# Three slots for the modulation weights of the mixing stages, one of them taken from the LRU gates' ring

## The chip, the cores and the metric

One core of a Trainium2 chip runs the program. The metric is the device time of one execution in microseconds (us); a lower time is better. The engines are TensorE (PE in the profile, its weight loads PEld), VectorE (DVE), ScalarE (ACT), GpSimd (POOL) and SyncE (SP), whose queue issues most of the transfers. Profile and runs are those of the kernel before the change.

## What is computed

A diffusion backbone of two layers over 512 latent tokens and 256 context tokens of 1024 features, all in float32. Every layer mixes tokens in two parallel groups (an S5 state-space group and a gated linear recurrence, the LRU), adds the result to the stream under a gate and normalises it, and then does the same with a gated convolutional FFN. Shifts, scales and gates of both halves come from the conditioning vectors through one large matrix per layer, `w_mod`, 1024 by 6144.

```
sh1, sc1, g1, sh2, sc2, g2 = split(silu(c) @ w_mod[l] + b_mod[l], 6)
proj  = modulate(x, sh1, sc1) @ w_in              # u (S5), x (LRU), g (gate of the LRU)
y_s5  = S5 scans of u, read out;  y_s5 = gelu(y_s5) * sigmoid(gelu(y_s5) @ w_glu + b)
y_lru = (forward scan + backward scan of a_t, b_t) * gelu(g)
x     = layer_norm(ALPHA * x + g1 * (concat(y_s5, y_lru) @ w_out))
x     = layer_norm(ALPHA * x + g2 * conv_ffn(modulate(x, sh2, sc2)))
```

In the LRU, `r` and `i` are sigmoids of two small products of the convolved x, `a = exp(-8 r softplus(..))`, `b = sqrt(1 - a*a) * i * x`, for each of two directions.

## The kernel before

Features lie on the 128 partitions and tokens along the free axis. A large product takes three matmuls (L170 to L172), with the high and low half of weights and activations; weights are loaded to one of two raw slots (L200) and split by ACT (L160, high) and DVE or POOL (L163, low).

The mixing stage of a layer goes over 8 head blocks of S5 (`prep`, `enter`, `leave`; DVE lines L722 to L738, readout matmuls L741 to L743). Each even-odd pair of blocks gives one tile of the S5 output, which is stored to DRAM by ACT's queue (`store_y`, L648) and loaded back transposed by SP's queue (L962) for the GLU (L966 activation, L977 sigmoid, L978 product). Between the blocks stand steps of the other work, one part of the string `FILL` per block: `u0` to `u3` and `x0` to `x3` project 128 columns of u or x, `l0` to `l3` run the LRU of a tile of 128 channels (gate matmuls L783, sigmoids L784, L794 to L803 on ACT, L798 to L813 on DVE with the scans L809, L810 and L812), `g0` to `g3` project the gate of a tile with its GELU (L925), and `s` is the GLU. When both LRU and gate of a tile are there, L936 multiplies them; after all steps, L163 splits the products into halves for the output projection.

The LRU writes its four gates and two more tensors per tile to a ring of slots, q0 to q5 and w6, w7. The result of a tile stays in the fifth of these six until L936 has read it.

Into this stage the modulation of the layer's second half is woven: `mods` (L304) makes the values of one third q of `w_mod`, in 16 steps of one 128 by 1024 load (L300, SP's queue, 512 KB) and four matmuls side by side (L185, L188), then adds the bias (L315), stores the gate rows (L318) and transposes the rest (L323, L328). q=1 and q=2 run here, 32 steps per layer; q=0 runs at the start or beside the FFN. The loads pass through the slots m0 and m1, which also take the bias row:

```
md_r = ring("m0", "m1")
filler = itertools.chain(*(mods(l, q, md_r, md_r, md_b, after=first_w) for q in (1, 2)))
```

In layer 0, w6 and w7 hold two tables of the S5 parameters (`s5_params`) from the start until the eight phase tables made from them (L575 to L578) are stored.

The order on each engine is made by a scheduler, from the order in which the code emits work and from priorities; within an engine, and within SP's queue, instructions start in that order, and one that waits holds up all behind it.

Of the kernel before, what the change touches and what calls it, by code (L numbers as in the profile page):

```python
# [45 lines left out]
LATE = 1  # L46
STEPS = 32
LOS = ("VVVVVVVV", "GVVVGVVV", "GVVVGVVV")
FILL = ('u1 x0 u2 u3|l0 x1||g0 l1 x2 g1|l2 x3|l3|g2|g3 s', 'x0 u1 u2 u3|l0 x1|g0 l1|x2 g1|l2 x3||l3|g3 g2 s')


@with_exitstack
def body(ctx: ExitStack, tc: tile.TileContext, a, out):
# [56 lines left out]
    def new(slot, shape, dt=F32):  # L110
        t, o, has = slots[slot]
        assert has == dt, (slot, dt)
        return carve(t, o, shape)
# [8 lines left out]
    def ring(*slots):  # L122
        it = itertools.cycle(slots)
        return lambda shape, dt=F32: new(next(it), shape, dt)
# [5 lines left out]
    def banks(*slots):  # L130
        it = itertools.cycle(slots)

        def get():
            s = next(it)
            return psum(s) if isinstance(s, str) else s
        return get
# [73 lines left out]
    class Stack:  # L210
        def __init__(self, t):
            self.t, self.p = t, 0
# [534 lines left out]
    class LRU:  # L747
        def __init__(self, l, cols, coef, keep):
            self.l, self.cols, self.coef, self.keep = l, cols, coef, keep
            where[0] = f"wg{l}"  # L750
            self.gates = ring(*(f"q{i}" for i in range(6)), "w6", "w7")

        def conv4(self, m, lat, ctxt):
            cw = lambda k: self.cols[:, 4 + 4 * k + m:5 + 4 * k + m]
# [78 lines left out]
    def bcast(t, src):  # L833
        load(t, src.partition_broadcast(128))
        return t
# [34 lines left out]
    for l in range(DEPTH):  # L870
# [10 lines left out]
        lat_b = ctx_b = gate_b = banks("p0", "p1", "p2")  # L881
        md_b = banks("p4")
        s5 = S5(l, prm)
        md_r = ring("m0", "m1")
        first_w = [None]
        filler = itertools.chain(*(mods(l, q, md_r, md_r, md_b, after=first_w) for q in (1, 2)))

        def proj(col, tag, do_ctx=True, parts=False):
            where[0] = f"{tag}{l}"
# [97 lines left out]
        steps = {"u": u_part, "x": x_part, "l": lru_part, "g": g_part, "s": glu}  # L987
        fill = [[(steps[x[0]], *map(int, x[1:])) for x in part.split()] for part in FILL[l].split("|")]
        emitted, loaded = {0}, {0}
# [42 lines left out]
        g1 = [bcast(gt[:, v], gd[l][0, v]) for v in range(1 if last else 2)]  # L1032
# [55 lines left out]
        g2 = [bcast(gt[:, v], gd[l][1, v]) for v in range(1 if last else 2)]  # L1088
# [102 lines left out]
        md_r = ring("m0", "m1")  # L1191
        md_b = banks(pvt[:, 1])
# [111 lines left out]
```

## Time and profile before

| | |
|---|---|
| median of 3 runs | 1739.45 us (1738.14 to 1739.81) |
| the profiled execution, its own time | 1738.61 us |
| its span, first to last instruction | 1736.8 us |
| PE busy | 1551.8 us (89%) |
| DVE busy | 1287.7 us (74%) |
| ACT busy | 672.1 us (39%) |
| POOL busy | 522.7 us (30%) |
| mean granted clock of PE | 0.938 of full speed |

The mixing stage of layer 0 runs from about 95 to 345 us of the span, that of layer 1 from about 1060 to 1292. Busy shares over the whole span mix stages with different limits, so a stage is read by its own stretch; a row of the waits says who waited for whom, and a row of the timeline gives start and duration of one instruction, with the idle time before it and its releaser in brackets.

### The profile page before, as it was taken

The numbers are of one execution on the slowest core, as the hardware profiler recorded it, in microseconds if no ns is written. First come the engines' busy times: TensorE is split into PE (matmuls) and PEld (weight loads), VectorE is DVE, ScalarE is ACT, GpSimd is POOL, SyncE is SP. The second block draws the span as 40 slices with busy tenths as digits, with TensorE's granted clock in tenths as the row PEclk, the third lists the DMA queues.
The fourth block names the chain that finished last, engine by engine and source line by source line (L and its number), as shares of the span: only waits on it lengthen the run. The fifth ranks groups of instructions, "written<-read, shape, count | busy, mean of one in ns | idle before, by whom it ended". The sixth has DMA issues, their size and how long they took to land. (4 is left out here: it accounts for less than half of the span.)

```text
span 1736.8 us, 22939 instructions
## 1 busy us (share of the span) xinstructions
PE 1551.8 (89%) x8824; PEld 1263.5 (73%) x8824; DVE 1287.7 (74%) x2244; ACT 672.1 (39%) x972; POOL 522.7 (30%) x328
## 2 busy tenths in 40 slices
PE   4997888498999999999999789989778999999996
PEld 1775666376988788887888668867456988888884
DVE  7998999368566997877689984888467575556587
ACT  3445566423633222222222236556651643323320
POOL 1000001318332222322326271000146444434374
PEclk8897888699899999999999998999879999999998
DMA  8365453522221212433334316765562233222231
GB/s 338 128 222 179 140 177 97 185 85 101 70 75 60 97 58 88 157 111 133 106 131 145 110 59 199 259 198 162 180 213 95 94 121 105 89 98 97 85 122 61
DMA packets 95358, 227.09 MB, mean 131 GB/s; under 512 B 28912, under 2 KB 39696, under 8 KB 95248
## 3 DMA queue, kind: packets, MB, share of 16 engines
q1 hardware_dynamic: 85456, 212.92, 36.6%
q10 hardware_dynamic: 9792, 12.71, 2.1%
q8 instruction: 69, 1.13, 0.3%
q14 instruction: 41, 0.34, 0.1%
HBM read 194.50 MB, written 31.10 MB: 130 GB/s over the span
## 5 line engine op out<-in xcount | busy, mean ns | idle before, releaser
L170 PE MATMUL banks<-ar,ar 128*128 128x512 f32 (+2 forms) x2152 | 774.9, 365 | 49.4 <-ACT ar L160 32.1
L171 PE MATMUL banks<-ar,ar 128*128 128x512 f32 (+2 forms) x2152 | 774.9, 361 | 16.8 <-DVE ar L396 13.1
L172 PE MATMUL banks<-ar,ar 128*128 128x512 f32 (+2 forms) x2152 | 767.8, 360 | 1.3 <-DVE ar L163 1.3
L163 POOL TENSOR_TENSOR ar<-ar,ar 128x1024 fp32r<-128x1024 f32 x148 | 364.9, 2473 | 672.8 <-ACT ar L160 596.1
L170 PEld LDWEIGHTS banks<-ar,ar 128*128 128x128 f32 x2152 | 411.1, 193 | 127.9 <-ACT ar L160 35.6
L171 PEld LDWEIGHTS banks<-ar,ar 128*128 128x128 f32 x2152 | 413.9, 192 | 80.8 <-DVE ar L396 15.1
L172 PEld LDWEIGHTS banks<-ar,ar 128*128 128x128 f32 x2152 | 413.8, 193 | 63.6 <-DVE ar L163 2.5
L160 ACT ACTIVATE ar<-ar 128x1024 fp32r<-128x1024 f32 (+2 forms) x248 | 238.9, 981 | 488.4 <-PE banks L171 212.3
L1143 DVE SCALAR_TENSOR_TENSOR ar<-banks,cols,ar 128x441 f32<-128x441 f32 (+2 forms) x352 | 243.6, 692 | 41.7 <-ACT ar L1138 35.1
L1177 DVE TENSOR_TENSOR ar<-banks,ar 128x512 f32<-128x512 f32 x160 | 109.4, 687 | 106.5 <-PE banks L172 104.5
L163 DVE TENSOR_TENSOR ar<-ar,ar 128x512 fp32r<-128x512 f32 (+2 forms) x100 | 113.6, 1148 | 81.0 <-ACT ar L160 64.3
L185 PE MATMUL banks<-ar,cond 128*32 128x256 f32 x192 | 65.9, 450 | 42.2 <-DMA ar<-in_w_mod_dram 42.2
L1150 ACT ACTIVATE ar<-ar,cols 128x768 f32<-128x768 f32 (+1 forms) x44 | 36.6, 831 | 130.5 <-DVE ar L1143 93.7
L826 POOL TENSOR_TENSOR ar<-ar 128x512 f32<-128x512 f32 x40 | 63.2, 1585 | 68.4 <-DVE ar L822 67.7
L185 PEld LDWEIGHTS banks<-ar,cond 128*32 128x32 f32 x192 | 16.2, 117 | 78.7 <-DMA ar<-in_w_mod_dram 59.6
L704 POOL MEMSET ar<- 128x8 f32 x16 | 1.9, 121 | 217.8 <-DVE ar L727 105.0
L188 PE MATMUL banks<-ar,cond 128*32 128x256 f32 x576 | 66.9, 450 | 0.0
L783 PE MATMUL banks<-ar,ar 128*128 128x512 f32 (+1 forms) x128 | 55.5, 563 | 10.3 <-ACT ar L925 5.7
L384 PE MATMUL banks<-ident,ar 128*128 128x128 f32 x176 | 36.0, 348 | 30.9 <-ACT ar L358 15.5
L396 DVE TENSOR_TENSOR ar<-ar,ar 128x256 fp32r<-128x256 f32 (+1 forms) x64 | 32.8, 531 | 31.8 <-ACT ar L395 31.7
L1138 ACT ACTIVATE ar<-banks,cols 128x512 f32<-128x512 f32 x44 | 29.9, 680 | 66.9 <-PE banks L172 66.8
L822 DVE TENSOR_TENSOR ar<-banks,ar 128x512 f32<-128x512 f32 x60 | 40.5, 681 | 18.7 <-PE banks L172 18.7
(243 smaller groups left out, 1723.3 us busy)
## 6 DMA issues: line engine op xcount, KB each, us to landing
ar<-in_w_mod_dram SPq DMA_DIRECT2D x96, 512.0 KB
ar<-in_ffn_w_up_dram SPq DMA_DIRECT2D x88, 512.0 KB
ar<-in_ffn_w_down_dram SPq DMA_DIRECT2D x44, 512.0 KB
ar<-in_w_in_dram SPq DMA_DIRECT2D x24, 512.0 KB
tabd<-ar SPq DMA_DIRECT2D x16, 512.0 KB
ar<-tabd SPq DMA_DIRECT2D x16, 512.0 KB
csd<-ar SPq DMA_DIRECT2D x16, 384.0 KB
ar<-csd SPq DMA_DIRECT2D x16, 384.0 KB
```

Source lines behind the costliest of these rows:

```text
L160: S.activation(hi, src, AF.Copy)
L163: return lo_eng.tensor_tensor(lo, src, hi.bitcast(F32), op=SUB)
L170: PE.matmul(ps, wh, xh, start=first and k == 0, stop=False)
L171: PE.matmul(ps, wh, xl, start=False, stop=False)
L172: PE.matmul(ps, wl, xh, start=False, stop=last and k == nk - 1)
L185: ins = PE.matmul(*args, **kw)
L188: ins = PE.matmul(*args, **kw)
L783: PE.matmul(gp, w[:, d, i, :], xc[:, o:o + n], start=True, stop=True)
L822: V.tensor_tensor(tmp, ps, g[:, cs], op=MUL)
L826: G.tensor_tensor(xs_t[:, cs], xs_t[:, cs], tmp, op=ADD)
L1143: inst[0] = V.scalar_tensor_tensor(av[:, yo, xo], uv[:, yi, xi], tap(1 + dy, 1 + dx, ch), av[:, yo, xo], op0=MUL, op1=ADD)
L1177: V.tensor_tensor(acc, ps, acc, op=ADD)
```

## The change

Three edits. The modulation loads of the mixing stages pass through three slots, m0, m1 and w7, and three are fetched ahead instead of two. The ring of the LRU's gates loses w7 and has seven slots. And `FILL` puts `g2` ahead of `l3` in both layers (in layer 1 it stood in the last part): the ring of seven reuses the slot of a tile's result in the next tile's call, so L936 of tile 2 has to come ahead of the LRU of tile 3.

```
-FILL = ('u1 x0 u2 u3|l0 x1||g0 l1 x2 g1|l2 x3|l3|g2|g3 s', 'x0 u1 u2 u3|l0 x1|g0 l1|x2 g1|l2 x3||l3|g3 g2 s')
+FILL = ('u1 x0 u2 u3|l0 x1||g0 l1 x2 g1|l2 x3|g2|l3|g3 s', 'x0 u1 u2 u3|l0 x1|g0 l1|x2 g1|l2 x3|g2|l3|g3 s')
...
-            self.gates = ring(*(f"q{i}" for i in range(6)), "w6", "w7")
+            self.gates = ring(*(f"q{i}" for i in range(6)), "w6")
...
-        md_r = ring("m0", "m1")
+        md_r = ring("m0", "m1", "w7")
...
-        filler = itertools.chain(*(mods(l, q, md_r, md_r, md_b, after=first_w) for q in (1, 2)))
+        filler = itertools.chain(*(mods(l, q, md_r, md_r, md_b, 3, after=first_w) for q in (1, 2)))
```

No instruction of arithmetic and no transfer is added or removed; the order changes on PE, DVE, ACT and SP's queue, and on POOL it stays.

DVE at the end of layer 0's mixing, before. L807 to L813 belong to the LRU of tile 3, L722 to L725 begin the last S5 block.

```order
L807 TENSOR_TENSOR ar_83<-ar_83,ar_88 128x768
L807 TENSOR_TENSOR ar_85<-ar_85,ar_89 128x768
L684 TENSOR_TENSOR ar_68<-banks,dd_114 128x16
L809 SCALAR_TENSOR_TENSOR ar_88<-ar_82,ar_83 128x256
L812 SCALAR_TENSOR_TENSOR ar_89<-ar_84,ar_85 128x768
L810 SCALAR_TENSOR_TENSOR ar_88<-ar_82,ar_88,ar_83 128x512
L722 TENSOR_TENSOR ar_68<-ar_68 128x768
L723 TENSOR_TENSOR ar_68<-ar_68 128x768
L813 TENSOR_TENSOR ar_88<-ar_88,ar_89 128x768
L163 TENSOR_TENSOR ar_67<-ar_68,ar_67 128x1024
L724 TENSOR_TENSOR ar_68<-ar_68 128x384
L725 TENSOR_TENSOR ar_68<-ar_68 128x384
```

After: the last block ends with L735 to L738, and the LRU of tile 3 goes on behind it.

```order
L737 TENSOR_TENSOR ar_68<-ar_68 64x4x32
L738 TENSOR_TENSOR ar_68<-ar_68 64x4x64
L804 SCALAR_TENSOR_TENSOR ar_82<-ar_88,ar_82 128x768
L807 TENSOR_TENSOR ar_85<-ar_85,ar_81 128x768
L163 TENSOR_TENSOR ar_66<-ar_68,ar_66 128x768 x2
L807 TENSOR_TENSOR ar_80<-ar_80,ar_82 128x768
L163 TENSOR_TENSOR ar_66<-ar_68,ar_66 128x768
L809 SCALAR_TENSOR_TENSOR ar_81<-ar_84,ar_85 128x256
L315 TENSOR_TENSOR ar_68<-banks,ar_68 128x512
L812 SCALAR_TENSOR_TENSOR ar_82<-ar_88,ar_80 128x768
L810 SCALAR_TENSOR_TENSOR ar_81<-ar_84,ar_81,ar_85 128x512
L328 TENSOR_SCALAR modc_23_105<-banks 128x4x2 x2
```

What moved: both L807, one of the two L804, the scans and L813 of tile 3 stand behind the last block, and so do two of the halves (L163 of 128x768) that stood ahead of its L735.

SP's queue at the same place, before. L962 loads the S5 output (the second one here is the last tile), L1037 a tile of x, L834 a gate row.

```order
L200 DMA ar_68<-in_w_out_s_dram 128x1024 [waits Pool_49]
L1037 DMA ar_68<-in_x_dram 128x1024 [waits DMAHW7_49,DVE_49]
L834 DMA ar_68<-gd_107 128x1024 [waits DMAHW0_49,PE_49]
L200 DMA ar_68<-in_w_out_s_dram 128x1024 [waits DMAHW4_49,DMAHW1_49,Pool_49]
L962 DMA ar_68<-yd 128x8x96 [waits DMAHW2_49,PE_49]
L834 DMA ar_68<-gd_107 128x1024 [waits DMAHW3_49,PE_49]
L1037 DMA ar_68<-in_x_dram 128x1024 [waits DVE_49]
L200 DMA ar_68<-in_w_out_lru_dram 128x1024 [waits DMAHW6_49,Pool_49]
L200 DMA ar_68<-in_w_out_lru_dram 128x1024 [waits DMAHW7_49,DMAHW1_49,Pool_49]
L962 DMA ar_68<-yd 128x8x96 [waits DMAHW5_49,DMAHW0_49]
```

After, up to the last L962:

```order
L318 DMA gd_107<-ar_68 2x256 [waits DMAHW6_49,DVE_49]
L318 DMA gd_107<-ar_68 2x256 [waits DMAHW7_49]
L318 DMA gd_107<-ar_68 2x256 [waits DMAHW0_49]
L318 DMA gd_107<-ar_68 2x256 [waits DMAHW1_49]
L200 DMA ar_68<-in_w_out_s_dram 128x1024 [waits DMAHW2_49,Pool_49]
L200 DMA ar_68<-in_w_out_s_dram 128x1024 [waits DMAHW3_49,Pool_49]
L1037 DMA ar_68<-in_x_dram 128x1024 [waits DMAHW4_49,DVE_49]
L962 DMA ar_68<-yd 128x8x96 [waits DMAHW5_49]
```

What moved: the last L962 now stands behind the gate rows of step q=2 (L318) and ahead of the loads of `w_out_lru`; the third L1037, directly ahead of it, waits for DVE.

ACT in layer 1, around and behind L794 of tile 3, before. L925 is the GELU of a gate projection, L160 a high half.

```order
L160 ACTIVATE ar_67<-ar_68 128x1024
L925 ACT_TABLE_LOAD
L925 ACTIVATE ar_68<-banks 128x512
L795 ACT_TABLE_LOAD
L795 ACTIVATE ar_7621<-ar_7621,lru_st_9046,coef_106_3713 128x768
L160 ACTIVATE ar_66<-ar_68 128x512 x2
L795 ACTIVATE ar_7623<-ar_7623,lru_st_9046,coef_106_3713 128x768
L160 ACTIVATE ar_66<-ar_68 128x1024
L925 ACT_TABLE_LOAD
L925 ACTIVATE ar_68<-banks 128x512
L801 ACTIVATE lru_st_9054<-ar_7623 128x1
L964 ACTIVATE glu_st_9200<-ar_68 128x1
```

After:

```order
L794 ACTIVATE ar_7620<-ar_7623,lru_st_9081,coef_106_3713 128x768
L794 ACTIVATE ar_7621<-ar_7627,lru_st_9081,coef_106_3713 128x768
L160 ACTIVATE ar_66<-ar_68 128x512 x2
L795 ACT_TABLE_LOAD
L795 ACTIVATE ar_7623<-ar_7623,lru_st_9081,coef_106_3713 128x768
L160 ACTIVATE ar_66<-ar_68 128x512
L795 ACTIVATE ar_7627<-ar_7627,lru_st_9081,coef_106_3713 128x768
L160 ACTIVATE ar_66<-ar_68 128x1024 x2
L925 ACT_TABLE_LOAD
L925 ACTIVATE ar_68<-banks 128x512
L801 ACTIVATE lru_st_9089<-ar_7627 128x1
L964 ACTIVATE glu_st_9201<-ar_68 128x1
```

What moved: one L925 with its table load is no longer between L794 and L803; it stands ahead of tile 3's sigmoids. On PE the corresponding projection stands ahead of tile 3's gate matmuls, of which no projection's matmuls now stand between the first and the last; and all steps of `mods` stand ahead of the GLU's products, where before five stood among them. In layer 0, PE has two steps of `mods` ahead of the first S5 blocks, as before, and the other 30 behind the load that waits for w7.

## Rows read from the trace of the kernel before

**Rows 1.** Busy times by stretch: window, then engines' busy us (instructions), PEclk, DMA share, GB/s.

```profile
95.00:310.00 215.00, 173.62 (x1283) 132.74 (x1276) 200.45 (x316) 117.48 (x185) 7.37 (x15) 0.86 0.51 162
310.00:331.50 21.50, 3.53 (x17) 3.28 (x16) 1.71 (x2) 9.77 (x13) 9.32 (x4) 0.50 0.79 264
...
1195.00:1262.00 67.00, 51.72 (x312) 34.03 (x312) 38.03 (x56) 42.93 (x59) 4.80 (x3) 0.84 0.58 187
1262.00:1292.00 30.00, 20.82 (x140) 16.83 (x141) 16.75 (x17) 16.87 (x25) 16.11 (x6) 0.74 0.48 167
```

**Rows 2.** Waits of PE in 95:310, 1195:1262, 1262:1292: total us, times, longest.

```profile
PE banks L185 <- DMA ar<-in_w_mod_dram: 20.0, 11, 3.6
...
PE banks L185 <- DMA ar<-in_w_mod_dram: 10.7, 4, 3.6
...
PE banks L185 <- DMA ar<-in_w_mod_dram: 3.7, 1, 3.7
```

**Rows 3.** Groups of DVE in 284:313: xcount | busy us, mean ns | idle before.

```profile
L807 DVE TENSOR_TENSOR ar<-ar,ar 128x768 f32<-128x768 f32 x2 | 1.8, 952 | 0.0
...
L812 DVE TENSOR_TENSOR_SCAN ar<-ar,ar 128x768 f32<-128x768 f32 x1 | 1.7, 1733 | 0.0
L810 DVE TENSOR_TENSOR_SCAN ar<-ar,ar,ar 128x512 f32<-128x512 f32 x1 | 1.3, 1260 | 0.0
```

**Rows 4.** Timeline of DVE, end of layer 0's mixing: start us, us, instruction.

```profile
299.59 3.10 DVE L732 TENSOR_TENSOR ar<-ar 128x768 f32<-128x768 f32 x1
302.61 3.96 DVE L163 TENSOR_TENSOR ar<-ar,ar 128x768 fp32r<-128x768 f32 x2
...
308.48 0.42 DVE L738 TENSOR_TENSOR ar<-ar 64x256 f32<-64x256 f32 x1
...
311.66 0.96 DVE L163 TENSOR_TENSOR ar<-ar,ar 128x768 fp32r<-128x768 f32 x1 [0.91 <-ACT ar L160]
```

**Rows 5.** Timelines of SP's queue and of ACT, same place.

```profile
322.69 0.39 SPq L962 DMA_DIRECT2D ar<-yd  x1
...
327.39 3.41 ACT L966 ACTIVATE ar<-ar,glu_st 128x768 f32<-128x768 f32 x4
```

**Rows 6.** Timeline of ACT, end of layer 1's mixing.

```profile
1242.75 0.69 ACT L784 ACTIVATE ar<-banks,cols 128x512 f32<-128x512 f32 x1 [4.26 <-PE banks L783]
...
1253.78 1.28 ACT L925 ACT_TABLE_LOAD   x1
1255.08 0.60 ACT L925 ACTIVATE ar<-banks 128x512 f32<-128x512 f32 x1
...
1261.19 2.56 ACT L966 ACTIVATE ar<-ar,glu_st 128x512 f32<-128x512 f32 x4
```

**Rows 7.** Timeline of PE, gates of tile 3 and GLU of layer 1.

```profile
1229.25 1.19 PE L783 MATMUL banks<-ar,ar 128*128 128x256 f32 x2 [1.68 <-issue]
...
1241.69 1.02 PE L783 MATMUL banks<-ar,ar 128*128 128x512 f32 x2
...
1264.84 0.80 PE L170 MATMUL banks<-ar,ar 128*128 128x256 f32 x2 [3.72 <-ACT ar L160]
...
1276.73 0.40 PE L185 MATMUL banks<-ar,cond 128*32 128x256 f32 x1 [3.68 <-DMA ar<-in_w_mod_dram]
...
1291.27 0.38 PE L323 MATMUL banks<-ident,ar 128*128 128x128 f32 x2
```

**Rows 8.** Timeline of POOL, end of layer 0's mixing.

```profile
298.93 5.95 POOL L163 TENSOR_TENSOR ar<-ar,ar 128x1024 fp32r<-128x1024 f32 x2 [24.51 <-ACT ar L160]
```

**Rows 9.** Timeline of DVE, layer 1: the scan of tile 2.

```profile
1224.73 1.26 DVE L810 TENSOR_TENSOR_SCAN ar<-ar,ar,ar 128x512 f32<-128x512 f32 x1
```

**Rows 10.** SP's queue: one table store (timeline); w_mod loads in 95:158, 150:310.

```profile
153.98 0.33 SPq L578 DMA_DIRECT2D csd<-ar  x1
...
L300 SPq DMA_DIRECT2D ar<-in_w_mod_dram x12: 327/328/1159, 107.7 to 149.6; - x12
...
L300 SPq DMA_DIRECT2D ar<-in_w_mod_dram x16: 327/330/431, 163.7 to 257.1; - x16
```

## The prediction

> **What bounds the kernel now.** The change touches only the two mixing stages, so the page's shares for the whole program (TensorE busy for nearly nine tenths of the span) decide little, and I read stage by stage. First the busy times by stretch [rows 1]. In layer 0, from 95 to 310 us, VectorE (DVE) works 200.45 of 215 us; TensorE (PE) works 173.62. DVE is the limit there, with only 14.55 us of idle time, while from 310 to 331.5 both engines stand almost still. In layer 1 the end of the stage, 1195 to 1292, has no engine that is full: PE 51.72 of 67 and 20.82 of 30, DVE less. So that end is a chain of waits.
>
> Second, the waits of PE for modulation weights [rows 2]: 20.0 us in eleven waits in layer 0, 10.7 and 3.7 us at the end of layer 1. This is what a third slot speaks to. What they are worth differs by stage: in layer 0 PE isn't the limit, so most of the 20.0 us cost nothing; in layer 1 a wait sits in the chain unless something else ends later.
>
> Third, the end of layer 0. On DVE the LRU of tile 3 has its instructions ahead of the last S5 head block (durations in [rows 3]); that block's last DVE instruction ends at 308.48 + 0.42 = 308.9, and DVE's last work of the stage at 311.66 + 0.96 = 312.6 [rows 4]. Then the block's result goes to DRAM and comes back transposed: the last load is issued at 322.69, and the GLU's first activation starts at 327.39 [rows 5]. For those 15 us DVE has nothing to do. So DVE work that is not needed by the last block is done at the wrong time: behind the block it would be free.
>
> Fourth, the end of layer 1. On ScalarE (ACT) the last sigmoid of tile 3's gates runs at 1242.75, after a wait of 4.26 us for PE; the GELU of a gate projection with its table load comes at 1253.78 and 1255.08, and the GLU's activation starts at 1261.19 [rows 6]. On PE the gate matmuls of tile 3 start at 1229.25, but the last pair only at 1241.69, since a projection's matmuls stand between; the GLU's products run from 1264.84 until the step's transposes at 1291.27 [rows 7], 26.4 us, with five modulation steps inside, one of them after a wait of 3.68.
>
> **The change, part by part.** Two things are moved: the slots, and gate projection 2 ahead of the LRU of tile 3. The arithmetic is the same, and so is the count of transfers. The scheduler then writes another order, and that order is what I cost.
>
> *Layer 0, DVE.* Behind the last block's final instruction there now stand one L804, both L807, L809, L812, L810, L813, and two low halves (L163) that stood ahead. With 0.95 for each of the four of L807's form (L804 and L813 have its size), 1.73 and 1.26 for the scans [rows 3], about 0.6 for L809 (an estimate, a third of L812, whose columns are three times as many) and the two halves between 1.9 (two of 0.96 alone) and the 3.96 that they took [rows 4], this is 4 x 0.95 + 1.73 + 1.26 + 0.6 + (1.9 to 3.96) = 9.3 to 11.4 us. The block ends that much sooner, at 297.5 to 299.6.
>
> What is late next: SP's queue. The last load of the GLU's input now stands behind a load of x that waits for DVE's last low half, and DVE's total is unchanged, so that half ends at 312.6 as before. The load can go at about 313. The other bound is the store's path, 322.69 - 308.9 = 13.8 us behind the block's end, so 311 to 313.4. Both give some 9.5 us less than 322.69. From this I take 2.5 us, because the order is new and DVE's idle time, now 14.55 in 215 [rows 1], may grow by anything from 0 to half again (7). Layer 0: 7 us, between 2 and 9.5.
>
> *The two halves beside GpSimd.* L732 took 3.10 us here [rows 4], other tensor operations of that size 0.95 [rows 3]; it ran beside two GpSimd conversions that began at 298.93 and lasted 5.95 us [rows 8], and the L163 pair behind it was stretched as well. In my sum this contention is left where it is, since DVE works without a break through both places. The Trainium skill, "SBUF — State Buffer", section "Who interferes with whom", says that a VectorE instruction with two SBUF inputs and a GpSimd instruction that reads SBUF block each other fully. By that rule more of the moved instructions, nearly all of this kind, may be held up than those that were before; the price is in the second rival.
>
> *Layer 1, gates and ACT.* Gate projection 2, 24 matmuls, goes ahead of tile 3's gates. PE was waiting there: 10.7 us between 1195 and 1262 [rows 2], so the projection, some 5.5 us, is covered; without that cover it would delay the gates by its length. In return the matmuls between the gates are gone: the 4.26 us that the last sigmoid waited [rows 6] fall away, of which I take 4. Then, between the sigmoids and the GLU's activation, ACT has one GELU and one table load less: 1255.08 - 1253.78 + 0.60 = 1.9 us. Together 5.9.
>
> *Layer 1, steps in the GLU.* All modulation steps now stand ahead of the GLU's products, six of them in a row where PE has to wait for ACT anyway. Inside the 26.4 us they cost at least the wait of 3.7 [rows 2] and at most 7.7 (with five steps of two passes, 0.40 us each [rows 7]). Part of it hid other waits: 3, between 0 and 7.7. Layer 1: 9 us, between 4 and 13.5.
>
> *One slot fewer for the gates' ring.* Now the second gate of a tile waits for the first scan of the tile before. In layer 1 that scan ended at 1224.73 + 1.26 = 1226.0 [rows 9], and the gates start at 1229.25 [rows 7], so 3.2 us of cover hide it; I count nothing. If the scan comes over 3.2 us later against the gates, each further microsecond lands on the chain.
>
> *The slot itself in layer 0.* w7 holds a table of S5 parameters until the last of the eight phase tables is made, whose store was issued at 153.98 [rows 10]. Counting SP's order, four of the stage's 32 loads come before that point and 28 behind it. Twelve loads took 107.7 to 149.6, that is 41.9/11 = 3.8 us each; sixteen took 163.7 to 257.1, 93.4/15 = 6.2 us each [rows 10]. The last two steps stand on PE ahead of the block's readout, so all 28 have to land by 299: (299 - 4 - 154)/28 = 5.0 us each. I take a value near 3.8: that was the pace when steps were asked for one after another; the 6.2 was the pace at which they were asked for. So no price, and the start 40 us later is free.
>
> Sum: 7 + 9 = 16 us off the profiled execution's 1738.6, that is 1722.6. Its span is 1736.8, and it lies 0.84 below the median of the runs, 1739.45, so 1723.5 for a median.
>
> **The rivals.** *Only one gain arrives* (0.22): in layer 0 the conversions on GpSimd, or idle time on DVE, take the 7 us back. For it speaks L732's 3.10; another pair of 5.95 us in the moved work would leave 1 of 7. Against it: that pair was already paid once. Time: 1739.5 - 1 - 9 = 1729.5. This is also the case that the page on SBUF would make of it.
>
> *No change* (0.12): the order holds only on paper, the waits for weights turn into waits for scans and halves of the same length, and both ends stay where they are: 1739, within 3.5 us. For it: in layer 0 DVE, not PE, is the limit. Against it: the block's end and the GLU's activation are moved by order, not by waits.
>
> *Slower* (0.14): the supply in layer 0. If 28 loads need 6.2 us each [rows 10], the last lands at 154 + 28 x 6.2 + 4 = 331.6, against a readout that now begins about 308; even if SP's gaps give some back, say 4 us, the stage ends 20 later, less layer 1's 9: 1750. It decides from 5.7 us a load: 154 + 28 x 5.7 + 4 = 317.6, where layer 0 loses what layer 1 gains. For it: in layer 0 SP has all the other loads in the same queue, and w_mod loads that wait for a slot hold them up.
>
> *All waits vanish* (0.04): 20.0 + 10.7 + 3.7 = 34.4 us [rows 2], 1705. Against it stands DVE's 200.45 of 215 in layer 0. The Trainium skill, "Perfetto Trace Analysis", section "Optimization Strategy", takes gaps that repeat for a stretch on the engine that should be saturated as a sign of too few buffers; read so, the third slot gives the whole sum, but in layer 0 that engine is DVE, not PE.
>
> **How the numbers follow.** My forecast, both ends shorter, has 0.48; its own range is 1715 to 1731. With the rivals: faster by over 0.2% (3.5 us, about what a measurement of this kernel can tell from no change) 0.48 + 0.22 + 0.04 = 0.74, same 0.12, slower 0.14. The bounds of the terms, 9.5 + 13.5 at best, give 1716.5, with some of the waits beyond the chains 1710; upwards the range takes in no change and the first of the slower case, 1741.
>
> **What would show it.** Right: in layer 0 the last yd load some 7 to 10 us sooner, with the LRU of tile 3 on DVE running while the store and load are under way; in layer 1 no modulation step inside the GLU, whose products take under 23 us, and the GLU's activation some 6 us sooner against the last scan of tile 2; PE's waits for w_mod under 20 us in all. Wrong: PE waiting for w_mod right ahead of the last block's readout in layer 0, more idle time on DVE between 150 and 300, or gate matmuls that wait for scans.

## The result: 1708.1 us, and the profile after

The changed kernel takes 1708.1 us (median of 4 runs, 1704.91 to 1709.21) against 1738.8 us for the kernel before in the same comparison; the ratio is 0.9823, 95% interval 0.9804 to 0.9843. That is 30.7 us less, about twice the forecast of 16, and below the range given. The profiled execution took 1707.04 us with a span of 1705.3; the mean granted clock of PE is 0.945 where it was 0.938.

The busy times of the changed kernel by stretch, the windows of [rows 1] (those of layer 1 moved to the same place of the program; columns as there):

```profile
95.00:310.00 215.00, 169.44 (x1273) 128.91 (x1271) 201.50 (x314) 125.03 (x191) 10.64 (x17) 0.88 0.56 178
310.00:331.50 21.50, 15.65 (x75) 14.84 (x76) 9.15 (x6) 14.70 (x20) 11.54 (x5) 0.76 0.44 153
1167.00:1234.00 67.00, 54.99 (x370) 36.53 (x368) 47.06 (x68) 46.27 (x63) 4.76 (x3) 0.91 0.67 215
1234.00:1264.00 30.00, 20.33 (x107) 18.24 (x108) 19.12 (x20) 17.84 (x27) 13.10 (x5) 0.70 0.29 96
```

From 310 to 331.5 PE now works 15.65 us where it stood almost still (3.53), and its granted clock there is 0.76 instead of 0.50: the layer's end has come forward into this window. PE's waits for modulation weights, in 95:310 and in 1167:1234 (total us, times, longest), against 20.0 and 10.7 in [rows 2]; in the GLU of layer 1 there is none left:

```profile
PE banks L185 <- DMA ar<-in_w_mod_dram: 2.5, 1, 2.5
...
PE banks L185 <- DMA ar<-in_w_mod_dram: 5.2, 4, 3.2
```

The end of layer 0's mixing on DVE (timeline; answers to [rows 4]):

```profile
288.34 0.42 DVE L738 TENSOR_TENSOR ar<-ar 64x256 f32<-64x256 f32 x1
...
292.27 3.10 DVE L807 TENSOR_TENSOR ar<-ar,ar 128x768 f32<-128x768 f32 x1
295.29 3.09 DVE L163 TENSOR_TENSOR ar<-ar,ar 128x768 fp32r<-128x768 f32 x1
...
301.15 1.25 DVE L810 TENSOR_TENSOR_SCAN ar<-ar,ar,ar 128x512 f32<-128x512 f32 x1
...
305.37 0.96 DVE L163 TENSOR_TENSOR ar<-ar,ar 128x768 fp32r<-128x768 f32 x1 [0.91 <-ACT ar L160]
```

The last S5 block ends at 288.8, before at 308.9: 20.1 us sooner. The LRU of tile 3 runs behind it, as expected. DVE's last work ends at 306.3, before at 312.6: 6.3 us sooner, with the same work (201.50 against 200.45 us in the window). SP's queue and ACT at this place ([rows 5]):

```profile
306.36 0.33 SPq L1037 DMA_DIRECT2D ar<-in_x_dram  x1
306.74 0.43 SPq L962 DMA_DIRECT2D ar<-yd  x1
...
311.33 3.41 ACT L966 ACTIVATE ar<-ar,glu_st 128x768 f32<-128x768 f32 x4
```

The last yd load stands right behind a load of x that waited for DVE's last half, as the prediction had it, but at 306.74 and not at 313: 16.0 us sooner than before. The GLU's activation is 16.1 us sooner, layer 0's FFN and most of layer 1's S5 blocks keep 18 to 20 of it, and the rest comes at the end of layer 1's mixing. There, on ACT ([rows 6]):

```profile
1217.40 0.69 ACT L784 ACTIVATE ar<-banks,cols 128x512 f32<-128x512 f32 x1 [0.39 <-PE banks L783]
...
1227.04 1.28 ACT L925 ACT_TABLE_LOAD   x1
1228.34 0.60 ACT L925 ACTIVATE ar<-banks 128x512 f32<-128x512 f32 x1
...
1233.50 2.56 ACT L966 ACTIVATE ar<-ar,glu_st 128x512 f32<-128x512 f32 x4
```

The GLU's activation in layer 1 starts at 1233.50, 27.7 us sooner than before; the span ends 31.5 sooner.

Last, SP's queue early in layer 0, the loads of `w_mod` (L300) and the stores of the phase tables (L578), which [rows 10] show as they were:

```profile
87.67 0.81 SPq L300 DMA_DIRECT2D ar<-in_w_mod_dram  x2
...
123.80 18.92 SPq L578 DMA_DIRECT2D csd<-ar  x3
145.67 0.33 SPq L300 DMA_DIRECT2D ar<-in_w_mod_dram  x1
149.65 0.32 SPq L578 DMA_DIRECT2D csd<-ar  x1
154.86 1.28 SPq L300 DMA_DIRECT2D ar<-in_w_mod_dram  x3
```

Between 88 and 145 us there is no load of modulation weights any more: the first that goes to w7 waits for the table in that slot. Before, 12 loads went out between 107.7 and 149.6.

### The profile page after: what moved, and what is told of

It reads as the page before. It is cut to its first block, busy times and chain, and to the rows that moved or that the text cites. A ratio compares the mean times of both kernels' runs of the same rounds, so it can differ in the third digit from the quotient of the medians.

```text
span 1705.3 us, 22948 instructions
## 1 busy us (share of the span) xinstructions
PE 1540.7 (90%) x8824; PEld 1255.2 (74%) x8824; DVE 1288.9 (76%) x2244; ACT 676.1 (40%) x976; POOL 524.0 (31%) x328
## 4 chain that ended last, share of the span: by engine, by line
PE 55%; DVE 20%; ACT 4%; POOL 3%; issue 3%; DMA 2%; POOLq 0%; ACTq 0%; SPq 0%; DVEq 0%
PE banks L170 17%; PE banks L171 16%; PE banks L172 16%; DVE ar L1143 3%; DVE ar L163 2%; POOL ar L826 2%; PE banks L783 1%; PE banks L185 1%; DVE ar L830 1%; DVE ar L1177 1%; POOL ar L163 1%; DVE ar L822 1%; ACT ar L160 1%; DVE ar L1182 1%; PE banks L702 1%
## 5 line engine op out<-in xcount | busy, mean ns | idle before, releaser
L170 PE MATMUL banks<-ar,ar 128*128 128x512 f32 (+2 forms) x2152 | 775.8, 366 | 58.2 <-ACT ar L160 30.4
L171 PE MATMUL banks<-ar,ar 128*128 128x512 f32 (+2 forms) x2152 | 777.1, 362 | 17.0 <-DVE ar L396 12.7
L163 POOL TENSOR_TENSOR ar<-ar,ar 128x1024 fp32r<-128x1024 f32 x148 | 366.4, 2483 | 646.5 <-ACT ar L160 555.1
L160 ACT ACTIVATE ar<-ar 128x1024 fp32r<-128x1024 f32 (+2 forms) x248 | 238.8, 981 | 492.9 <-PE banks L171 206.9
L163 DVE TENSOR_TENSOR ar<-ar,ar 128x512 fp32r<-128x512 f32 (+2 forms) x100 | 114.1, 1155 | 70.5 <-ACT ar L160 51.4
L185 PE MATMUL banks<-ar,cond 128*32 128x256 f32 x192 | 61.4, 432 | 12.9 <-DMA ar<-in_w_mod_dram 12.8
L188 PE MATMUL banks<-ar,cond 128*32 128x256 f32 x576 | 62.3, 432 | 0.0
L710 POOL MEMSET ar<- 128x4 f32 x16 | 1.7, 105 | 178.3 <-ACT ar L709 178.3
L1138 ACT ACTIVATE ar<-banks,cols 128x512 f32<-128x512 f32 x44 | 29.9, 679 | 66.9 <-PE banks L172 66.7
L783 PE MATMUL banks<-ar,ar 128*128 128x512 f32 (+1 forms) x128 | 51.9, 531 | 4.1 <-ACT ar L784 1.7
```

The source lines that it names most:

```text
L160: S.activation(hi, src, AF.Copy)
L163: return lo_eng.tensor_tensor(lo, src, hi.bitcast(F32), op=SUB)
L170: PE.matmul(ps, wh, xh, start=first and k == 0, stop=False)
L171: PE.matmul(ps, wh, xl, start=False, stop=False)
L185: ins = PE.matmul(*args, **kw)
L188: ins = PE.matmul(*args, **kw)
```

## The experiments

Times are medians; ratios are to the kernel before in the same comparison; instants are those of the one profiled execution of each kernel. e4, e6, e14, e15, e16 and e18 leave out a dependence or a part of the modulation, so they compute something else than the others. Three instants of layer 0 tell where a kernel stands: the start of the last DVE instruction (L738) of the third and of the eighth S5 block, and the issue of the last yd load (L962). Where an edit adds lines, these are L739 to L741 and L963 to L966 in that kernel.

| kernel | slots, start of the steps in layer 0 | 3rd block | 8th block | last yd load | time |
|---|---|---|---|---|---|
| before | two, early | 182.4 | 308.5 | 322.7 | 1738.8 |
| the change | three, late | 168.1 | 288.3 | 306.7 | 1708.1 |
| e1 | two, early | 179.7 | 316.7 | 329.9 | 1746.0 |
| e2 | two, early | 178.3 | 315.9 | 330.3 | 1742.4 |
| e4 | three, late | 168.8 | 286.6 | 301.4 | 1710.9 |
| e5 | three, early | 180.2 | 316.6 | 329.7 | 1732.3 |
| e6 | two, early, half the bytes | 174.4 | 308.2 | 321.9 | 1732.5 |
| e7 | two, early, GpSimd's queue | 184.2 | 315.9 | 328.0 | 1747.2 |
| e9 | two, late | 169.9 | 314.1 | 328.6 | 1745.0 |
| e10 | three, late by another hold | 168.9 | 282.9 | 299.8 | 1708.4 |
| e11 | two, late | 169.7 | 311.8 | 326.9 | 1734.5 |
| e12 | three, from 119 us | 171.1 | 303.6 | 315.1 | 1716.2 |
| e14 | three, early, an eighth of the bytes | 175.4 | 292.0 | 312.6 | 1709.4 |
| e15 | three, early, matmuls of 16 columns | 172.9 | 302.2 | 316.9 | 1712.3 |
| e16 | two, late, half the bytes | 169.1 | 306.7 | 319.4 | 1735.1 |
| e18 | two, late, an eighth of the bytes | 168.4 | 298.4 | 312.4 | 1728.3 |

### The parts: order, ring, layers

`e1_order` has the new order alone, `e2_order_ring` the order and the ring of seven, both with two slots; `e3_layer0` and `e3_layer1` make the whole change in one layer.

```diff
 e1, e2
+FILL = (... '... l2 x3|g2|l3|g3 s', '... l2 x3|g2|l3|g3 s')
 e2 alone
+self.gates = ring(*(f"q{i}" for i in range(6)), "w6")
```

> Only the order of the steps is changed (gate of tile 2 ahead of the LRU of tile 3 in both layers); two slots for the modulation weights, eight slots in the ring. Theory A (the order alone gives the gain, since the LRU's vector work leaves the stretch in which VectorE is full): at or below 1716 us, the first layer's last yd load some 15 us sooner than before, PE's waits for w_mod in the first layer still about 20 us. Theory B (the late modulation weights held up PE, and through PE the ScalarE and VectorE; the prediction put that at nothing): the order alone gives what the prediction gave it, 7 us in the first layer and 6 in the second, 1722 to 1732 us; the rest comes with the slot.

> The new order and a ring of seven slots for the LRU's gates, but still two slots for the modulation weights (w7 lies idle). Theories A and B both: within 3 us of the kernel with the new order alone, since the ring's wait lies under 3.2 us of cover. If instead one slot fewer changes the order in which the LRU's work comes and that is part of the gain or of a loss, it stands over 3 us away from it. What separates it from the whole change is the slot alone: under A at most 3 us, under B 10 to 17 us.

> The whole change in the first layer alone, the second layer as before. The two traces put 18 to 20 us of the gain into the first layer: 1719 to 1722 us. If part of the first layer's gain needs the second layer's change, or the clock pays for it later, it is 1723 us or more. The prediction's own term for this layer (7 us) would give 1732.

> The whole change in the second layer alone, the first layer as before. The two traces put 10 to 12 us here: 1727 to 1730 us; the prediction's term was 9 us. With the kernel changed in the first layer alone the gains should add up to some 30 us; if they do not, one layer's gain depends on the other.

Measured: e1 1746.0 us, ratio 1.0045 (1.0029 to 1.0061); e2 1742.4, 1.0019 (1.0007 to 1.0030); layer 0 alone 1715.0, 0.9870 (0.9852 to 0.9888); layer 1 alone 1726.7, 0.9933 (0.9915 to 0.9951). Both theories are wrong about the order: by itself it makes the kernel slower. Its last S5 block on DVE (timeline of e1):

```profile
295.42 1.25 DVE L810 TENSOR_TENSOR_SCAN ar<-ar,ar,ar 128x512 f32<-128x512 f32 x1
...
300.27 5.89 DVE L727 TENSOR_TENSOR_SCAN ar<-ar 128x384 f32<-128x384 f32 x2
...
313.32 2.56 DVE L738 TENSOR_TENSOR ar<-ar 64x256 f32<-64x256 f32 x1
...
316.68 0.42 DVE L738 TENSOR_TENSOR ar<-ar 64x256 f32<-64x256 f32 x1
```

The scan of tile 3 (L810) stands ahead of the block's scans (L727) although `FILL` has `l3` a block later than before. So the order on the engines that the prediction read does not come from `FILL` alone. e2 is 3.6 us under e1, just beyond the 3 that both theories allowed. From e2 to the whole change only the slot is added, with the third load ahead, and 34 us go. Layer 0 gives 23.7 us and layer 1 12.0; together they give 30.7, so the two gains overlap by some 5.

### The slot alone, and the slot early

`e4_slot_old_order` keeps the old order; `e5_early_slot` keeps the whole change but frees w7 from the start; `e6_half_loads` and `e7_pool_queue` are the kernel before with smaller loads and with another queue.

```diff
 e4 (to before)
+self.gates = ring(*(f"q{i}" for i in range(6)), "w6")
+md_r = ring("m0", "m1", "w7")
+... mods(l, q, md_r, md_r, md_b, 3, after=first_w) ...
+V.tensor_mul(ge[0][:, m, 0:ntok], ge[0][:, m, 0:ntok], (ge[0][:, m] if m == 2 else hs[m])[:, 0:ntok])
 e5 (to the change)
+slots["e0"] = (slots["e"][0], slots["e"][1], F32)
+slots["e1"] = (slots["e"][0], slots["e"][1] + 768, F32)
-params = s5_params(0, "t", ("a2", "t0"), ("w6", "w7"), ...
+params = s5_params(0, "t", ("a2", "t0"), ("e0", "e1"), ...
 e6 (to before)
+n = 512 if after else 1024
+mod_load[0] = load(raws[-1][:, 0:n], a["w_mod"][..., ... + n])
 e7 (to before)
+mod_load[0] = (G.dma_start if after else load)(raws[-1], ...)
```

> Three slots and a ring of seven in the old order of the steps. A ring of seven would let the LRU of tile 3 write over the result of tile 2 before gate 2 has read it, so gate 2's product reads its own gate twice instead of that result (same work on VectorE, one dependence fewer; the output is not the reference's). The new order without the slot was 3.7 to 7.3 us slower than before, the whole change 31 faster. Theory S (the slot gives the gain by itself, the order only makes it possible): 1704 to 1716 us. Theory J (order and slot are needed together: the order moves the LRU of tile 3 out of the way only if the last S5 block can come early, and that needs the slot): half or less of the gain, 1724 to 1739 us.

> The whole change, with the first layer's phase tables in the memory of the gates (free until 163 us) in place of w6 and w7, so that the third slot is free from the first step on and not from about 145 us. Theory S or J by supply alone: the same or some us faster than the whole change, 1700 to 1709 us. Theory L (the gain in the first layer comes from the late slot, which by its place in the queue holds the modulation steps back until after the tables are stored, so that the early stretch is free for the S5 blocks): most of the first layer's 20 us is lost, 1718 to 1730 us.

> The kernel before (old order, two slots, ring of eight) with half of each modulation weight load of the mixing stages left out (512 of 1024 columns; the rest of the slot holds old values, so the output is not the reference's). TensorE's waits for w_mod (20 us in the first layer before) should shrink to a quarter or less without any slot. Supply theory (those waits are what the slot cures): a gain of 15 us or more, 1705 to 1724 us. If it is the freedom in the order of the S5 blocks and not the waits themselves: under 8 us, 1731 us or more.

> The kernel before with the modulation weight loads of the mixing stages issued by GpSimd, so that a load that waits for its slot holds up nothing in SyncE's queue (before, SyncE waited 35 us for the steps' matmuls ahead of such loads, with csd and td loads behind them). Queue theory (what is behind the blocked loads in SyncE's queue, the csd and td loads of the S5 blocks, is what is late): a gain of 10 to 25 us, 1714 to 1729 us. Supply theory (the slot's own load time, PE's wait on it): within 4 us of before, or slower since GpSimd's issue is slower.

Measured: e4 1710.9 us, 0.9845 (0.9822 to 0.9868); e5 1732.3, 0.9969 (0.9954 to 0.9985); e6 1732.5, 0.9959 (0.9945 to 0.9974); e7 1747.2, 1.0066 (1.0040 to 1.0091). Theory S holds for the order (e4 has the gain in the old one; gate 2's dependence on the LRU is cut there, so the order's own worth is not shown to the microsecond). The supply theory falls: with half the bytes e6 gains 5.6 us, where it had 15 or more. The queue theory finds no support, but e7 does not clear SP's queue either: GpSimd's queue stood at these loads for 58.2 us between 95 and 345, with its own work behind them. And e5 decides between S and L: with the third slot free from the start 5.9 us are left, less than the 12 that layer 1's change gives alone, so layer 0 gains nothing. PE of e5 waits 11.6 us for modulation weights in 95:310 (its line for the step is L187), 8.4 fewer than before, and yet its last block ends 8 us later: those waits were not what layer 0 paid for.

```profile
PE banks L187 <- DMA ar<-in_w_mod_dram: 11.6, 9, 2.9
```

The loss begins early in the chain of blocks (DVE of e5, then of the change, end of the third block):

```profile
180.24 0.42 DVE L740 TENSOR_TENSOR ar<-ar 64x256 f32<-64x256 f32 x1
```

```profile
168.09 0.42 DVE L738 TENSOR_TENSOR ar<-ar 64x256 f32<-64x256 f32 x1
```

e5's eighth block is 28.2 us behind the change's; 12.2 of them are there by the third block, right behind the stretch in which the change loads no modulation weights, and 16.5 by the seventh (289.35 against 272.81).

### Late steps with two slots and with three

`e9_hold` is the kernel before, `e10_early_hold` is e5 and `e11_order_hold` is e1, each with layer 0's modulation loads, but for the first two, queued on SP behind the last csd store; `e12_early_hold4` is e10 with the fourth store in place of the last.

```diff
+..., csd_store, slow = ..., [None, None], itertools.chain([0, 0], itertools.repeat(1))
...
+csd_store[hb > 7] = nc.sync.dma_start(csd[l, hb], ...)
...
+with behind(after and (csd_store[0] if l == 0 and next(slow) else after[0])):
```

> The kernel before (old order, two slots, ring of eight), with the first layer's modulation weight loads but for the first two queued on SyncE behind the last csd store (about 154 us), as the third slot's table does in the whole change. Theory L (late steps are what frees the first layer): the third S5 block ends near 168 us and not at 181, the last near 288 and not 308, and the time falls by most of the 20 us that the first layer gave: 1716 to 1722 us. If two slots are then too slow for the 28 loads that are left (they came at 3.8 us each where nothing else held them, so 107 us from 154, which is soon enough; at 6.2 us each they would end at 328), the GLU becomes late: 1740 us or more. If late steps are not the cause: 1735 to 1740 us.

> Three slots free from the start (the phase tables in the gates' memory), which lost most of the gain, and the same hold of the loads behind the last csd store. Theory L: the gain comes back, 1704 to 1712 us. If moving the tables to the gates' memory was itself the loss: it stays at 1728 to 1736 us.

> The new order of the steps alone (two slots, ring of eight; slower than before by itself) with the hold. Theory L: the last S5 block ends near 288 us here too, and the second layer keeps what it has without the slot (nothing or a loss): 1714 to 1724 us. If the hold needs the third slot: 1735 us or more. Against the kernel with the hold in the old order, this tells what the order is worth once the steps are late.

> As the run with three early slots and the hold, but held only behind the fourth of the eight csd stores (about 123 us in place of 154). Theory L with the early stretch as a whole to be kept free: part of the gain, 1710 to 1725 us. If what matters is only that the first burst of some ten steps (105 to 125 us) does not stand ahead of the first blocks: all of it, 1704 to 1710 us.

Measured: e9 1745.0 us, 1.0042 (1.0028 to 1.0055); e10 1708.4, 0.9823 (0.9803 to 0.9844); e11 1734.5, 0.9978 (0.9964 to 0.9991); e12 1716.2, 0.9878 (0.9857 to 0.9899). e10 brings all of the gain back, so the tables' place was not e5's loss; the late start is part of the gain. But e9 shows that it is not enough. Busy times of e9 in layer 0 (columns as in [rows 1]):

```profile
95.00:160.00 65.00, 49.49 (x346) 41.91 (x345) 62.36 (x113) 30.55 (x53) 0.44 (x4) 0.84 0.43 138
160.00:220.00 60.00, 50.93 (x394) 35.25 (x393) 55.52 (x84) 36.73 (x57) 0.44 (x4) 0.94 0.61 191
220.00:290.00 70.00, 56.51 (x410) 38.09 (x411) 57.29 (x91) 39.98 (x62) 0.54 (x5) 0.85 0.56 177
```

and of the change:

```profile
95.00:160.00 65.00, 50.61 (x338) 42.13 (x337) 62.60 (x111) 30.87 (x51) 0.43 (x4) 0.84 0.44 140
160.00:220.00 60.00, 49.77 (x388) 35.90 (x388) 57.90 (x88) 37.02 (x57) 0.54 (x5) 0.90 0.58 191
220.00:290.00 70.00, 66.27 (x531) 48.65 (x530) 65.69 (x103) 50.90 (x77) 0.43 (x4) 0.97 0.59 185
```

To 160 us they are alike (DVE 62.36 and 62.60), and the third block ends at 170 and 168. Then e9 falls back: from 220 to 290 DVE works 57.29 us against 65.69, PE 56.51 against 66.27, and PE waits 10.9 us for modulation weights, where the change waits none (from 160 on 16.2 against 2.5). SP's queue shows the same. Its waits at the loads of `w_mod` (L300) in 160:300, in e9 and then in the change (total us, times, longest):

```profile
SPq L300 <- PE banks L188: 32.0, 21, 5.5
SPq L300 <- DMA ar<-in_w_mod_dram: 23.5, 14, 3.4
```

```profile
SPq L300 <- PE banks L188: 26.3, 15, 3.1
SPq L300 <- DMA ar<-in_w_mod_dram: 2.8, 3, 1.8
```

That is 55.5 against 29.1 us, with the blocks' own loads behind them in the queue; DVE of e9 waits 4.4 us for csd there, which the change does not. How much e9 loses by this queue and how much by PE's own waits no run separates. So the gain of layer 0 needs both: the steps must leave the early stretch, and nearly all of them (28 in the change, 30 in e9) then have to go through the late one, which two slots do only at the blocks' cost. e11, with the new order, ends just under the 1735 us that its expectation set for a hold that needs the third slot. The last yd load says it in one view of the table: 322.7 to 330.3 in every two-slot kernel with full loads, early or late, and with three early slots and full steps; 299.8 to 306.7 with three late ones; 315.1 half way (e12).

### What the early steps cost, and why two slots fail

`e14_early_small_loads` and `e15_early_small_steps` are e5 with layer 0's modulation loads cut to 128 columns and with its step matmuls cut to 16 (e14 also clears w7 at the start); `e16_hold_half_loads` and `e18_hold_small_loads` are e9 with loads of 512 and of 128 columns.

```diff
 e14, e18 (e16: 512)
+n = 128 if after and l == 0 else 1024
+mod_load[0] = load(raws[-1][:, 0:n], a["w_mod"][..., ... + n])
 e14 alone
+G.memset(new("w7", [128, 1024]), 0.0)
 e15
+raw, mc = raws.pop(0), 16 if after and l == 0 else 256
+... ps[32 * t:32 * t + 32, h, 0:mc], cond[:, kc, :], raw[:, 256 * t:256 * t + mc] ...
```

> The run with three slots free from the start (1732 us), with the first layer's modulation loads cut to 128 of 1024 columns (an eighth of the bytes; the slots keep old values or zeros, so the output is not the reference's). If the early steps cost by the bytes that their loads put on the DMA engines and in SyncE's queue, the gain of the late start comes back without it: 1704 to 1712 us, third S5 block at 168 us. If they cost by their matmuls and their place in TensorE's queue: 1722 us or more, third block near 179 us.

> The same run with three early slots and full loads, but with the first layer's modulation matmuls cut from 256 to 16 columns each (the output is not the reference's). If the early steps cost by TensorE's time: 1704 to 1714 us, third block at 168 us. If they cost by bytes or by waits for the loads: 1722 us or more.

> Two slots, old order, the loads held behind the last csd store (1745 us), with each of the first layer's modulation loads cut to half its columns (the output is not the reference's). If two slots fail there because the 28 late loads are too slow (TensorE waited 16 us for them and the S5 blocks fell behind from 170 us on): the first layer's gain comes back, 1714 to 1724 us. If it is not the supply: 1736 us or more.

> Two slots, old order, the hold, with each of the first layer's modulation loads cut to 128 of 1024 columns (the output is not the reference's). With half the columns the time was 1735 us, where 1714 to 1724 had been expected from the supply. If the supply's bytes are still what is left of the loss: 1714 to 1722 us. If two slots cost by the turn itself (a load can only be issued when the matmuls two steps back are done, whatever its size), so that the steps stand among the S5 blocks at a pace of two a turn: 1728 us or more.

Measured: e14 1709.4 us, 0.9841 (0.9814 to 0.9868), last yd load at 312.6; e15 1712.3, 0.9849 (0.9824 to 0.9873), 316.9; e16 1735.1, 0.9983 (0.9970 to 0.9996), 319.4; e18 1728.3, 0.9944 (0.9926 to 0.9963), 312.4. In time, taking the bytes away or taking PE's time away each brings back 20 to 23 of e5's 24 us. But both kernels make all 32 steps of the layer smaller, the late ones too, and layer 0 itself shows less. The last yd load, at 329.7 in e5 and 299.8 in e10, comes back by 17.1 us in e14 and 12.8 in e15; the start of the GLU's last sigmoid, at 362.7 in e5 and 337.3 in e10, by 14.1 (348.6) and 12.7 (350.0). So neither is the cost alone: either one less brings back about half of the 25.4 us. Behind the GLU the two kernels win another 6 to 7 us on e10, where their edits change no instruction; that stays open.

With two late slots the bytes explain a good half. e9 has nothing of layer 1's change, so it is held against that of layer 0 alone (1715.0): of these 30.0 us e16 brings back 9.9 and e18 16.7, and PE of e18 still waits 6.7 us in six waits. The other 13.3 us may go with the turn of two slots, in which a load can be issued only behind the matmuls two steps back; that the turn is the reason is argued from what is left, and no run shows it by itself (e18 also has the old order and ring).

### A version that might have been faster

`e17_late_layer1` is e10 with layer 1's steps begun only at the fourth S5 block.

```diff
+MODS = (2, 3)
+SPR = (2, 2)
+if (l > 0 and hb > 2) or (l == 0 and hb > 1):
```

> A version that may beat the change: three slots free from the start and the hold in the first layer (1708 us), and in the second layer the modulation steps begin only with the fourth S5 block, two or three at a time (in its place in the program TensorE is full, 69.6 of 70 us, from 1030 to 1100 us, and has 13 us to spare from 1200 to 1240). If late steps help where an engine that bounds the stretch is freed: 5 to 12 us, 1696 to 1704 us. If the steps then come too late and stand before the GLU: 1708 us or more.

Measured: 1710.4 us, 0.9836 (0.9813 to 0.9859). No gain over the change. In the profiled execution layer 1's last S5 block ends later than in e10 (L740 at 1210.1 against 1193.1). PE's stretch from 1030 to 1100 stayed full (68.56 of 70 us, in e10 69.62), and the third block was no sooner (1104.5 against 1103.1), so what a freer stretch would give is not shown. No kernel here beats the change; e10 and e4 equal it within their intervals.

## Why the prediction was wrong about the size, point by point

**Layer 0: the step that failed.** The bound was right: the last yd load goes when DVE's last half is done, and the store's path ends sooner. Had DVE's last half stayed at 312.6, the gain would have been 322.7 - 313 = 9.7 us, the 9.5 of the prediction. From this it took 2.5 "because the order is new and DVE's idle time ... may grow by anything from 0 to half again". The idle time fell. Busy times of 95 to 290 before and then in the change (columns as in [rows 1]):

```profile
95.00:290.00 195.00, 166.01 (x1240) 126.21 (x1233) 180.57 (x294) 109.85 (x176) 1.41 (x13) 0.88 0.53 171
```

```profile
95.00:290.00 195.00, 166.65 (x1254) 126.68 (x1253) 186.19 (x301) 118.79 (x184) 1.41 (x13) 0.90 0.54 172
```

By 290 us DVE had done 180.57 us of work before and 186.19 in the change, and its last half came 6.3 sooner: 9.7 + 6.3 = 16.0, as measured, where 7 stood. The range allowed DVE's idle time no fall, so the term's own range of 2 to 9.5 missed it. Two more were won in the GLU itself, whose first sigmoid is 18.2 us sooner.

**Why it failed.** Two sentences carried it. "Most of the 20.0 us cost nothing" is borne out as far as e5 goes: it takes 8.4 of them away and layer 0 gains nothing. "The start 40 us later is free" was the mistake: the late start was priced by whether the loads still land in time, and never by what the early steps cost the S5 blocks. e5 against e10 prices it at 23.9 us in all (1732.3 - 1708.4), 29.9 us at the last yd load.

**The cause named was wrong as well.** The prediction read the LRU of tile 3 behind the last block and put it down to the order of the steps. e1 has that order in `FILL` and not on DVE; e4 has the old `FILL` and the new order on DVE. Nor is the order enough: e11, with two slots and late steps, has tile 3's scan behind the last block too, and its block ends no sooner than before (DVE of e4, then of e11):

```profile
286.57 0.42 DVE L738 TENSOR_TENSOR ar<-ar 64x256 f32<-64x256 f32 x1
...
293.02 1.26 DVE L810 TENSOR_TENSOR_SCAN ar<-ar,ar,ar 128x512 f32<-128x512 f32 x1
```

```profile
311.76 0.42 DVE L738 TENSOR_TENSOR ar<-ar 64x256 f32<-64x256 f32 x1
...
318.91 1.27 DVE L810 TENSOR_TENSOR_SCAN ar<-ar,ar,ar 128x512 f32<-128x512 f32 x1
```

Of the 20.1 us by which the change's last block is sooner, 7.3 are there at the end of the seventh (280.13 before, 272.81 now); the other 12.8 fall within the eighth, near the 9.3 to 11.4 that the prediction counted for the work moved behind it. So that sum was about right, but the edit that it was put down to was not the one that made it.

**The supply.** The 28 late loads went out from 145.7 to 272.7, 127/27 = 4.7 us each, under the 5.0 that the prediction needed and over the 3.8 that it took. With two slots late steps do fail (e9, 1745 us, without layer 1's change), but not as the rival "slower" has it: e9's 30 held loads were out by 280.9, from 151.2 on 4.5 us each, and not at 6.2; what was late was the blocks.

**Layer 1: right.** 9 us were forecast (4 to 13.5); the layer's change alone gave 12.0, with its interval 8.5 to 14.8 (1738.7 times 0.0049 and 0.0085). By its parts: from the last scan of tile 2 (1224.73 in [rows 9], now 1203.47) to the GLU's activation it was 36.5 us and is 30.0, 6.5 less where 5.9 stood. e1 has 29.0 there (1242.05 to 1271.06), so this part came with the order, as forecast, although in e1 the scan itself is later. The last sigmoid waits 0.39 us instead of 4.26, though another waits 2.13. Between the GLU's activation and its last sigmoid it was 32.2 and is 29.5, 2.7 less where 3 stood; no step is inside, and six stand where PE waits for ACT (below). A gain for which no term stood lies ahead of that scan: the lead over the kernel before was 18.3 us at the last sigmoid of layer 0's GLU and 21.3 at the scan, 3.0 more.

```profile
1228.19 0.52 PE L185 MATMUL banks<-ar,cond 128*32 128x256 f32 x1 [3.17 <-DMA ar<-in_w_mod_dram]
...
1236.63 0.80 PE L170 MATMUL banks<-ar,ar 128*128 128x256 f32 x2 [4.85 <-ACT ar L160]
```

**The ring with one slot fewer: right.** e2 differs from e1 in that alone and is not slower (1742.4 against 1746.0).

**The rivals.** "All waits vanish" gave 1705 and lies nearest, for the wrong reason: PE's waits for w_mod fell from 42.2 to 12.8 us over the kernel, but e5 shows that layer 0's gain is not their sum. The Trainium skill, "Perfetto Trace Analysis", section "Optimization Strategy", says that gaps which repeat on the engine that should be saturated can mean too little memory for the next tile; here more memory alone (e5) left layer 0 where it was. That does not speak against the sentence: the gaps were on PE, and the engine that this stage keeps busy is DVE, as the prediction held against this rival. "Only one gain" and its contention did not come: L807 and a half took 3.10 and 3.09 us beside GpSimd, as much stretch (4.3 us) as L732 and the pair had in [rows 4] (4.2).

## What to carry to other kernels

When a change delays some work, price the delay by what that work did to its neighbours where it stood, not only by whether it still comes in time. The test is a kernel that holds the work back, built with and without the other edits: here the hold alone lost (e9), the slot alone gave layer 0 nothing (e5), and both together gave it all (e10). Take the order that a scheduler writes as the answer to all edits together, and build the edits one by one before naming the one that made it. Before counting that an engine's idle time "may grow", give its fall a range too.

## What was not expected of the hardware

In e1 GpSimd's conversions fell on the last S5 block, the first two on its scans (timeline of GpSimd in e1):

```profile
296.56 8.79 POOL L163 TENSOR_TENSOR ar<-ar,ar 128x1024 fp32r<-128x1024 f32 x2 [22.67 <-ACT ar L160]
```

The scans L727 took 5.89 us there and 1.79 in the block before, while the two conversions themselves took 8.79, where one of that form takes 2.34 in the kernel before when it starts at 312.66 and DVE has nothing to do: both engines were held up, by 4.1 us each, and scans are too. Beside two later conversions an L735 took 2.69 us instead of 0.54 and an L738 2.56 instead of 0.42. The Trainium skill, "SBUF — State Buffer", section "Who interferes with whom", has it so that VectorE and GpSimd share a port pair as an exclusive lock; the trace agrees in that both engines lose and that the L735 and the L738 take 2.15 and 2.14 us longer, near one conversion's 2.34; which instruction locked out which it does not show. Together this is 4.1 + 2.15 + 2.14 = 8.4 us in e1's last block, against 4.2 in the kernel before (L732 and the pair behind it), so 4.2 of the 8.2 us by which e1's last block is later.
